# Half groups of down products in other places of a tile of up products

## The chip, the cores and the metric

The kernel runs on one core of one Trainium2 chip. The metric is the device time of one execution in microseconds; the lower the better. A time of the kernel before is the median of several executions, and one more execution was taken with the hardware profiler.

## The reference

The program is a two-layer trunk on 528 tokens (16 meta tokens and 512 real ones) of width 1024: a sparse attention layer, a differential attention layer, and behind each of them the same gated ConvFFN. The change lies in the ConvFFN alone:

```python
def conv_ffn(h, w_up, conv_w, conv_b, w_down):
    Tp = h.shape[1]
    u = h @ w_up
    up = jnp.pad(u, ((0, 0), (CONV_W - 1, 0), (0, 0)))
    c = conv_b + sum(up[:, j:j + Tp] * conv_w[j] for j in range(CONV_W))
    gate, val = jnp.split(c, 2, axis=-1)
    return (jax.nn.silu(gate) * val) @ w_down
```

Here w_up is 1024 x 5632 and w_down 2816 x 1024, all in float32.

## The kernel before

Everything is held with features on the partitions and tokens along the free axis. Every float32 product is made of three matmuls, from an upper and a lower part of each operand: upper times upper, lower times upper, upper times lower. The upper part is a cast by ScalarE (line 168, "hi"), the lower part the remainder, by VectorE (line 176, "lo").

A ConvFFN goes over 22 tiles f of 128 gate and 128 value columns of w_up. Tiles 0 and 1 are computed plainly. Tiles 2 to 21 are computed by up_pair, one after the other, which makes the gate and value columns for both halves of the tokens with seven products instead of eight (a scheme of Strassen's kind, from sums of weights, S12 and S34, and sums of inputs, TT). Each product is twelve matmuls of 264 columns (258 in layer 1), all on line 1240. In the order of the text they are P1 (line 1267, into g0), P5 (1272, into g1), P6 (1278, into v0), P2 (1282, into g0), P3 (1295, into v0), P4 (1299, into g1) and P7 (1307, into v0). g and v are tiles of 1024 columns in PSUM; g0 and v0 lie below column 512, g1 and v1 from it on. g and v take turns in two buffers, so the next tile's g takes the buffer of this tile's.

Between the products, other engines move partial sums: ScalarE copies g0 to v0 behind P1 (line 1270) and g1 to p behind P5 (1274); VectorE writes v0 + p to g1 behind P6 (1279) and to v1 behind P3 (1296). Behind P4 convolve reads g (ScalarE line 1328, then two steps of VectorE, line 1331), and behind P7 it reads v.

The finished tiles of the hidden layer are multiplied by w_down in groups, as soon as four of them are there: a group is one of eight output blocks of 128 rows times four hidden tiles. It comes in two halves. A half group is twelve matmuls of 256 and 272 columns in layer 0 and six of 512 columns in layer 1 (line 1374, into a PSUM tile dn). Behind the second half ScalarE copies dn to y (line 1409), and POOL issues a DMA that adds y to h in memory (line 1410). The function down_slots gives each group a slot: a late one in tiles 4 to 19 (the generator b), or a mid one in tiles 5 to 20 (the generator a). Each next(a) issues one half, and the third next(a) the copy and the DMA.

The order on TensorE, VectorE and ScalarE is the order of the text here, since up_pair is emitted under manual_schedule. Every engine runs its own queue in that order and waits by semaphores where another engine's result is needed, or a buffer that another one still uses.

Weights come through two objects: wt for the up weights and their sums, ws (wsm) for the down weights and the last quarter of the value weight. Each has three buffers for raw, for hi and for lo. early casts a coming unit on ScalarE, late makes its lower part on VectorE, done says that a unit is used up, and each of them may let SP issue the next load (line 115).

Of the kernel before, what the change touches and what calls it, by code (L numbers as in the profile page):

```python
# [229 lines left out]
def mm_cost(n):  # L230
    return n / 2400 + 0.003


class Trunk:
# [929 lines left out]
    def ffn(self, l):  # L1164
# [4 lines left out]
        wt, ws, x = self.wt, self.wsm, self.next_x  # L1169
# [5 lines left out]
        with self.pool("fp") as fp:  # L1175
# [61 lines left out]
            def product(out, w, wk, xs, xk, c0, first=True):  # L1237
                for k in range(4):
                    for p, (wi, xi) in enumerate(((0, 0), (0, 1), (1, 0))):
                        nc.tensor.matmul(out, w[wi][:, wk + k, :], xs[xi][:, xk + k, c0:c0 + N],  # L1240
                                         start=(first and k == 0 and p == 0), stop=(k == 3 and p == 2), skip_group_check=not first)
                    self.pe(3 * mm_cost(N))
                    self.poll()

            def up_pair(f):

                x0, x1 = x[0][2:], x[1][2:]
                off = 512 - mid
                more = f + 1 < NF
                n3, ns = wt.taken, ws.taken
                a, b = ((z.get(f) and down(*z[f])) or iter(()) for z in (at_mid, at_late))
                g = ps.tile([128, 1024], F32, tag="sp", name="g")
                g0, g1 = g[:, off + st0:512], g[:, 512:512 + N]
                for i in range(ns, ns + (f in at_mid) + (f in at_late) + 1):  # L1260
                    ws.early(i)
                before = rest.pop(f - 1, iter(()))
                next(before, None)
                while ws.half:
                    ws.late()
                G, S12 = wt.take(), wt.take()
                product(g0, G, 0, x0, 0, st0)
                v = ps.tile([128, 1024], F32, tag="sp", name="v")
                v0, v1 = v[:, off + st0:512], v[:, 512:512 + N]
                nc.scalar.copy(v0, g0)  # L1270
                next(before, None)
                product(g1, S12, 0, TT[0], 0, 0)
                p5 = fp.tile([128, 264], F32, tag="p", name="p5", bufs=2)[:, :N]
                nc.scalar.copy(p5, g1)
                if more:
                    wt.sum()
                next(a, None)
                product(v0, S12, 4, TT[1], 0, 0, False)
                nc.vector.tensor_tensor(g1, v0, p5, op=OP.add)  # L1279
                if more:  # L1280
                    wt.sum()
                product(g0, G, 4, x0, 4, st0, False)
                wt.done()
                wt.done()
                wt.early(n3 + 3)
                wt.late()
                wt.early(n3 + 4)
                next(a, None)
                next(a, None)
                if f in at_mid:  # L1290
                    ws.done()
                if f + 1 in at_mid:
                    ws.early(ws.taken + (f in at_late) + 1)
                S34 = wt.take()
                product(v0, S34, 0, TT[2], 0, 0, False)
                nc.vector.tensor_tensor(v1, v0, p5, op=OP.add)
                wt.late()
                ws.late()
                product(g1, S34, 4, x1, 4, mid - 264, False)
                wt.done()  # L1300
                convolve(g, f, 0, off)
                wt.early(n3 + 5)
                wt.late()
                next(b, None)
                nc.scalar.activation(conv[0][:, :n], conv[0][:, :n], AF.Silu)
                A22 = ws.take()
                product(v0, A22, 0, TT[3], 0, 0, False)
                convolve(v, f, 1, off)
                next(b, None)
                if f in at_late:  # L1310
                    ws.done()
                ws.done()
                rest[f] = finish_pair(f, conv[0], conv[1], b)
# [3 lines left out]
            def finish_pair(f, c, t, b):  # L1317
                nc.vector.tensor_tensor(c[:, :n], c[:, :n], t[:, :n], op=OP.mult)
                next(b, None)
                yield  # L1320
                split_acts(f, c)
                yield

            def convolve(u, f, e, off=240):
                j = f + NF * e
                w0, w1, w2, b = (par[:, cb + 44 * q + j:cb + 44 * q + j + 1] for q in range(4))
                t = conv[e] = fp.tile([128, T], F32, tag=f"c{e}", name=f"c{e}", bufs=2)
                nc.scalar.activation(t[:, :n], u[:, off + t0:off + T], AF.Identity, bias=b, scale=w2)
                for d, w in ((1, w1), (2, w0)):
                    z = d if l == 0 else 0  # L1330
                    nc.vector.scalar_tensor_tensor(t[:, z:n], u[:, off + t0 + z - d:off + T - d], w, t[:, z:n],  # L1331
                                                   op0=OP.mult, op1=OP.add)
# [66 lines left out]
            def down(p, m):  # L1399
                f0, f1 = self.PARTS[p]  # L1400
                t, w = new(), ws.take()
                for k in range(f1 - f0):
                    if k == (f1 - f0) // 2:
                        yield
                    block(t, w, f0 + k, k, cols, k == 0, k == f1 - f0 - 1)
                yield
                y = fp.tile([128, T], F32, tag="y", name="y", bufs=2)
                for c0, c1, o in cols:
                    nc.scalar.copy(y[:, c0:c1], part(t, c0, c1, o))  # L1409
                nc.gpsimd.dma_start(self.h[m][:, t0:T], y[:, :n], accum_op=OP.add)  # L1410
                yield
# [34 lines left out]
            at_late, at_mid = self.down_slots()  # L1446
# [9 lines left out]
            with self.tc.manual_schedule(engines=ENGINES):  # L1456
                for f in range(self.PLAIN, NF):
                    up_pair(f)
                for _ in rest.pop(NF - 1):
                    pass  # L1460
# [479 lines left out]
```

## Time and profile before

| | |
|---|---|
| runs of the kernel before | 1418.61, 1424.5 and 1425.96 us, median 1424.5 us |
| the profiled execution | 1420.5 us, of which the span of the program is 1418.7 us |
| busy over the span | TensorE 92%, VectorE 73%, ScalarE 51%, POOL 24% |
| granted clock of TensorE, mean over the span | 0.975 of full speed |
| chain that ended last | TensorE 79%, VectorE 12%, ScalarE 5% of the span |
| tiles by up_pair | from about 300 to 640 us (layer 0) and from about 1046 to 1380 us (layer 1) |

Matmuls overlap in the pipeline: a matmul's row lasts about 0.28 us, while the next one starts 0.12 us after it. So a pause of TensorE is read best from start to start; the idle time that the profile gives in brackets is shorter, since it counts from the end of the last row.

### The profile page before, as it was taken

What the parts mean: (1) busy time and instruction counts of PE and PEld (TensorE: products, weight loads), DVE (VectorE), ACT (ScalarE), POOL (GpSimd) and SP (SyncE); (2) the same over time, 40 slices, a digit from 0 to 9 for tenths busy, and PEclk for the clock granted to TensorE, in tenths of its full rate; (3) what the DMA queues carried; (4) which work ended last, traced back from release to release, by engine and by line L of the source; (5) the groups of instructions that cost most, each with busy time, mean ns of one, the idle gap of its engine ahead of it and who ended that gap; (6) DMA issues with size and microseconds to landing.
All of it is one profiled execution on the core that took longest, in us unless ns stands there. A gap on an engine that the chain in (4) does not pass through costs nothing.

```text
span 1418.7 us, 25157 instructions
## 1 busy us (share of the span) xinstructions
PE 1303.5 (92%) x9688; PEld 1239.2 (87%) x9688; DVE 1033.2 (73%) x2030; ACT 723.1 (51%) x1426; POOL 343.4 (24%) x398
## 2 busy tenths in 40 slices
PE   5999899888999999989899999999888999999988
PEld 4999889887999999989799999989887888888886
DVE  6599876788777777766757777775888777777763
ACT  4453555565555555544435655654564555555541
POOL 3404443400000000003454543444500000001100
PEclk9999899999999999999899999989999999999999
DMA  7312221222444444433223222213222444444432
GB/s 229 116 60 84 75 84 58 82 83 59 123 119 120 121 122 122 112 82 101 66 79 93 66 72 76 61 34 89 76 82 75 127 120 119 119 120 127 111 78 93
DMA packets 58519, 136.03 MB, mean 96 GB/s; under 512 B 7216, under 2 KB 16736, under 8 KB 58400
## 3 DMA queue, kind: packets, MB, share of 16 engines
q1 hardware_dynamic: 48432, 114.57, 25.6%
q0 software_dynamic: 9968, 19.87, 8.2%
q8 instruction: 76, 1.25, 0.4%
q14 instruction: 43, 0.35, 0.1%
HBM read 112.46 MB, written 4.91 MB: 83 GB/s over the span
## 4 chain that ended last, share of the span: by engine, by line
PE 79%; DVE 12%; ACT 5%; issue 3%; DMA 1%; POOL 1%; SPq 0%; ACTq 0%; DVEq 0%; POOLq 0%
PE lin L306 21%; PE g L1240 17%; PE dn L1374 17%; PE v L1240 12%; DVE c L1331 2%; PE stq L681 1%; PE pv L1119 1%; PE pv L1745 1%; DVE g L1279 1%; DVE lo L176 1%; ACT v L1270 1%; PE linh L306 1%; PE sa L1024 1%; ACT hi L168 1%; DVE xl L630 1%
## 5 line engine op out<-in xcount | busy, mean ns | idle before, releaser
L306 PE MATMUL lin<-xh,hi 128*128 128x256 f32 (+3 forms) x928 | 273.5, 300 | 13.0 <-DVE ht L547 5.9
L306 PE MATMUL lin<-xl,hi 128*128 128x256 f32 (+3 forms) x928 | 274.0, 296 | 2.3 <-DVE xl L630 2.1
L306 PE MATMUL lin<-xh,lo 128*128 128x256 f32 (+3 forms) x928 | 273.5, 296 | 0.0
L168 ACT CAST hi<-raw 128x1024 fp32r<-128x1024 f32 (+3 forms) x225 | 181.7, 823 | 168.4 <-PE v L1240 81.9
L1410 POOL DMA_DIRECT2D ht<-y x64 | 55.8, 872 | 623.2 <-ACT y L1409 615.9
L306 PEld LDWEIGHTS lin<-xh,hi 128*128 128x128 f32 (+1 forms) x928 | 180.7, 197 | 16.8 <-ACT xh L656 8.4
L176 DVE TENSOR_TENSOR lo<-raw,hi 128x512 fp32r<-128x512 f32 (+3 forms) x196 | 179.0, 928 | 19.8 <-ACT hi L168 16.9
L306 PEld LDWEIGHTS lin<-xl,hi 128*128 128x128 f32 (+1 forms) x928 | 182.6, 197 | 4.0 <-DVE xl L630 3.7
L306 PEld LDWEIGHTS lin<-xh,lo 128*128 128x128 f32 (+1 forms) x928 | 182.5, 197 | 0.0
L1240 PE MATMUL g<-xh,hi 128*128 128x264 f32 (+1 forms) x480 | 140.7, 293 | 30.8 <-DVE g L1279 24.1
L1374 PE MATMUL dn<-al,hi 128*128 128x256 f32 (+2 forms) x528 | 142.6, 320 | 0.0
L1374 PE MATMUL dn<-ah,lo 128*128 128x256 f32 (+2 forms) x528 | 142.3, 321 | 0.0
L1374 PE MATMUL dn<-ah,hi 128*128 128x256 f32 (+2 forms) x528 | 142.2, 321 | 0.0
L1240 PE MATMUL v<-Th,lo 128*128 128x264 f32 (+1 forms) x480 | 136.2, 284 | 0.0
L1240 PE MATMUL v<-Tl,hi 128*128 128x264 f32 (+1 forms) x480 | 136.0, 283 | 0.0
L1240 PE MATMUL v<-Th,hi 128*128 128x264 f32 (+1 forms) x480 | 135.8, 283 | 0.0
L1240 PE MATMUL g<-xh,lo 128*128 128x264 f32 (+1 forms) x480 | 135.8, 283 | 0.0
L1240 PE MATMUL g<-xl,hi 128*128 128x264 f32 (+1 forms) x480 | 135.7, 283 | 0.0
L1240 PEld LDWEIGHTS g<-xh,hi 128*128 128x128 f32 x480 | 90.4, 188 | 40.9 <-DVE g L1279 32.5
L168 ACT CAST hi<-S 128x1024 fp32r<-128x1024 f32 x80 | 83.5, 1043 | 49.5 <-PE g L1240 48.1
L176 DVE TENSOR_TENSOR lo<-S,hi 128x1024 fp32r<-128x1024 f32 x80 | 97.3, 1216 | 0.0
L1374 PEld LDWEIGHTS dn<-ah,lo 128*128 128x128 f32 x528 | 89.1, 188 | 7.5
(301 smaller groups left out, 3304.0 us busy)
## 6 DMA issues: line engine op xcount, KB each, us to landing
raw<-w_up SPq DMA_DIRECT2D x88, 512.0 KB, 3.6
raw<-w_down SPq DMA_DIRECT2D x64, 256.0 KB, 3.2
ht<-y POOLq DMA_DIRECT2D x32, 264.0 KB, 3.6
raw<-w_in SPq DMA_DIRECT2D x16, 512.0 KB, 3.5
raw<-w_kv SPq DMA_DIRECT2D x16, 512.0 KB, 3.6
ht<-y POOLq DMA_DIRECT2D x32, 256.0 KB, 3.6
raw<-w_down SPq DMA_DIRECT2D x16, 384.0 KB, 3.2
nb<-nbias SPq DMA_DIRECT2D x16, 264.0 KB, 2.7
```

The source lines that it names most:

```text
L168: nc.scalar.copy(hi[:, :n, :m], src)
L176: eng.tensor_tensor(lt[:, :n, :m], src, hi[:, :n, :m].bitcast(F32), op=OP.subtract)
L306: i = self.nc.tensor.matmul(o, w[wi][:, kw + k, :m], x[s][xi][:, kx + k, c0:HN[s]], start=(first and p == 0), stop=(last and p == 2))
L630: i = eng.tensor_tensor(xl[:, m, o:o + n], xfs[m][:, :n], xh[:, m, o:o + n].bitcast(F32), op=OP.subtract)
L681: self.nc.tensor.matmul(st[:, c:c + 2], sq[:, c0:c0 + 128], rhs, start=True, stop=True)
L1024: nc.tensor.matmul(s, q[:, c0:c0 + 128], k[:, k0:k1], start=(p == 0), stop=(p == 2))
L1119: nc.tensor.matmul(pv[:, :4 * nq], v[:, c, :], pp[:, :, :nq], start=(ci == 0 and p == 0), stop=(ci == nch - 1 and p == 2))
L1240: nc.tensor.matmul(out, w[wi][:, wk + k, :], xs[xi][:, xk + k, c0:c0 + N], start=(first and k == 0 and p == 0), stop=(k == 3 and p == 2), ...
L1270: nc.scalar.copy(v0, g0)
L1331: nc.vector.scalar_tensor_tensor(t[:, z:n], u[:, off + t0 + z - d:off + T - d], w, t[:, z:n], op0=OP.mult, op1=OP.add)
L1374: nc.tensor.matmul(part(t, c0, c1, o), w[wi][:, k, :], acts[f][ai][:, c0:c1], start=(first and p == 0), stop=(last and p == 2))
L1410: nc.gpsimd.dma_start(self.h[m][:, t0:T], y[:, :n], accum_op=OP.add)
```

## The change

A half group of the mid slot, which was issued between P5 and P6, is now issued between P1 and P5. The other half, which was issued between P2 and P3, is now issued between P6 and P2, and with it goes what followed it: the copies of dn to y, the done of the group's weights, and the cast of the next mid group's weights (ws.early). The lower part of these weights (ws.late) is made there too. Tiles without a mid group (2 to 4 and 21) keep their order on TensorE.

```diff
--- before.py
+++ after.py
@@ -1269,33 +1269,33 @@
                 v0, v1 = v[:, off + st0:512], v[:, 512:512 + N]
                 nc.scalar.copy(v0, g0)
                 next(before, None)
+                next(a, None)
                 product(g1, S12, 0, TT[0], 0, 0)
                 p5 = fp.tile([128, 264], F32, tag="p", name="p5", bufs=2)[:, :N]
                 nc.scalar.copy(p5, g1)
                 if more:
                     wt.sum()
-                next(a, None)
                 product(v0, S12, 4, TT[1], 0, 0, False)
                 nc.vector.tensor_tensor(g1, v0, p5, op=OP.add)
                 if more:
                     wt.sum()
+                next(a, None)
+                next(a, None)
+                if f in at_mid:
+                    ws.done()
+                if f + 1 in at_mid:
+                    ws.early(ws.taken + (f in at_late) + 1)
+                    ws.late()
                 product(g0, G, 4, x0, 4, st0, False)
                 wt.done()
                 wt.done()
                 wt.early(n3 + 3)
                 wt.late()
                 wt.early(n3 + 4)
-                next(a, None)
-                next(a, None)
-                if f in at_mid:
-                    ws.done()
-                if f + 1 in at_mid:
-                    ws.early(ws.taken + (f in at_late) + 1)
                 S34 = wt.take()
                 product(v0, S34, 0, TT[2], 0, 0, False)
                 nc.vector.tensor_tensor(v1, v0, p5, op=OP.add)
                 wt.late()
-                ws.late()
                 product(g1, S34, 4, x1, 4, mid - 264, False)
                 wt.done()
                 convolve(g, f, 0, off)
```

On TensorE, in layer 0, the end of P1 (matmuls into g from xl and xh) and what follows it. Before:

```order
L1240 MATMUL g_4871<-xl0_3497,hi_4763 128x264
L1240 MATMUL g_4871<-xh0_3496,lo_4764 128x264
L1240 MATMUL g_4871<-Th0_3425,hi_4769 128x264
L1240 MATMUL g_4871<-Tl0_3426,hi_4769 128x264
L1240 MATMUL g_4871<-Th0_3425,lo_4770 128x264
```

Now:

```order
L1240 MATMUL g_4871<-xl0_3497,hi_4785 128x264
L1240 MATMUL g_4871<-xh0_3496,lo_4786 128x264
L1374 MATMUL dn_4908<-ah_3707,hi_4767 128x256
L1374 MATMUL dn_4907<-ah_3707,hi_4767 128x272
L1374 MATMUL dn_4908<-al_3708,hi_4767 128x256
```

Behind P1 stood P5 (from Th and Tl); now a half group stands there.

On TensorE, in the same tile, the end of P6 (matmuls into v) and what follows it. Before:

```order
L1240 MATMUL v_4901<-Tl1_3428,hi_4769 128x264
L1240 MATMUL v_4901<-Th1_3427,lo_4770 128x264
L1240 MATMUL g_4871<-xh0_3496,hi_4763 128x264
L1240 MATMUL g_4871<-xl0_3497,hi_4763 128x264
L1240 MATMUL g_4871<-xh0_3496,lo_4764 128x264
```

Now:

```order
L1240 MATMUL v_4901<-Tl1_3428,hi_4791 128x264
L1240 MATMUL v_4901<-Th1_3427,lo_4792 128x264
L1374 MATMUL dn_4908<-ah_3990,hi_4767 128x256
L1374 MATMUL dn_4907<-ah_3990,hi_4767 128x272
L1374 MATMUL dn_4908<-al_3991,hi_4767 128x256
```

Behind P6 stood P2; now the second half group stands there, and P2 behind it.

On ScalarE, from the copy behind P5 to convolve of g (the cast from raw 128x1024 is the next tile's G, the one from S its S12, the one from raw 128x512 the next mid group's down weight). Before:

```order
L1274 COPY p_4513<-g 128x264
L168 CAST hi<-raw 128x1024
L168 CAST hi<-S_4515 128x1024
L1409 COPY y<-dn 128x256
L1409 COPY y<-dn 128x272
L168 CAST hi<-raw 128x512
L1328 ACTIVATE c_4617<-g,par 128x528
```

Now:

```order
L1275 COPY p_4527<-g 128x264
L1409 COPY y<-dn 128x256
L1409 COPY y<-dn 128x272
L168 CAST hi<-raw 128x512
L168 CAST hi<-raw 128x1024
L168 CAST hi<-S_4529 128x1024
L1328 ACTIVATE c_4617<-g,par 128x528
```

The copies to y and the cast of the down weight have moved ahead of the casts of G and S12.

On VectorE, from the sum behind P6 to convolve of g. Before:

```order
L1279 TENSOR_TENSOR g<-v,p_4513 128x264
L141 TENSOR_TENSOR S_4545<-raw,S_4515 128x512
L142 TENSOR_TENSOR S_4545<-raw 128x512
L176 TENSOR_TENSOR lo<-raw,hi 128x1024
L1296 TENSOR_TENSOR v<-v,p_4513 128x264
L176 TENSOR_TENSOR lo<-S_4515,hi 128x1024
L176 TENSOR_TENSOR lo<-raw,hi 128x512
L1331 SCALAR_TENSOR_TENSOR c_4617<-g,par,c_4617 128x527
```

Now:

```order
L1279 TENSOR_TENSOR g<-v,p_4527 128x264
L141 TENSOR_TENSOR S_4545<-raw,S_4529 128x512
L142 TENSOR_TENSOR S_4545<-raw 128x512
L176 TENSOR_TENSOR lo<-raw,hi 128x512
L176 TENSOR_TENSOR lo<-raw,hi 128x1024
L1297 TENSOR_TENSOR v<-v,p_4527 128x264
L176 TENSOR_TENSOR lo<-S_4529,hi 128x1024
L1331 SCALAR_TENSOR_TENSOR c_4617<-g,par,c_4617 128x527
```

The lower part of the down weight has moved from the place ahead of convolve to the place ahead of G's lower part; line 1296 is line 1297 in the changed file. On SP the same loads stand in another order: two of w_up and two of w_down in turn were issued in pairs, and are now issued one of a kind after one of the other. POOL's order is the same.

## Rows read from the trace of the kernel before

**Rows 1.** Busy time in two stretches; columns: stretch, length, PE, PEld, DVE, ACT, POOL, clock, DMA.
```profile
450.00:500.00 50.00, 46.69 (x373) 45.42 (x372) 37.61 (x53) 25.75 (x45) 5.18 (x6) 1.00 0.47 126
1200.00:1250.00 50.00, 47.22 (x317) 43.10 (x317) 36.81 (x53) 26.20 (x40) 4.35 (x5) 1.00 0.48 127
```

**Rows 2.** Who waited for whom on PE, whole span: us in total, times, longest.
```profile
PE g L1240 <- ACT v L1270: 27.5, 40, 1.7
PE g L1240 <- DVE g L1279: 24.1, 40, 0.8
```

**Rows 3.** Timeline of PE, layer 0, P1 to P5: start, length, instruction, idle before.
```profile
422.12 0.28 PE L1240 MATMUL g<-xh,lo 128*128 128x264 f32 x1
422.90 0.39 PE L1240 MATMUL g<-Th,hi 128*128 128x264 f32 x1 [0.50 <-ACT v L1270]
423.12 0.29 PE L1240 MATMUL g<-Tl,hi 128*128 128x264 f32 x1
```

**Rows 4.** Timeline of PE, layer 0, P6 to P2.
```profile
427.30 0.28 PE L1240 MATMUL v<-Th,lo 128*128 128x264 f32 x1
428.18 0.39 PE L1240 MATMUL g<-xh,hi 128*128 128x264 f32 x1 [0.60 <-DVE g L1279]
428.41 0.28 PE L1240 MATMUL g<-xl,hi 128*128 128x264 f32 x1
```

**Rows 5.** Timeline of PE, layer 1: a half group, P6 to P2, P1 to P5.
```profile
1200.56 0.39 PE L1374 MATMUL dn<-ah,hi 128*128 128x512 f32 x1
...
1201.95 0.28 PE L1240 MATMUL v<-Th,hi 128*128 128x258 f32 x1
...
1203.28 0.28 PE L1240 MATMUL v<-Th,lo 128*128 128x258 f32 x1
1204.15 0.39 PE L1240 MATMUL g<-xh,hi 128*128 128x258 f32 x1 [0.60 <-DVE g L1279]
...
1215.49 0.28 PE L1240 MATMUL g<-xh,lo 128*128 128x258 f32 x1
1216.26 0.39 PE L1240 MATMUL g<-Th,hi 128*128 128x258 f32 x1 [0.49 <-ACT v L1270]
```

**Rows 6.** Timeline of PE, layer 0, tile 3: P2 to P3, P5 to P6.
```profile
328.07 0.28 PE L1240 MATMUL g<-xh,lo 128*128 128x264 f32 x1
328.19 0.28 PE L1240 MATMUL v<-Th,hi 128*128 128x264 f32 x1
...
338.68 0.29 PE L1240 MATMUL g<-Th,lo 128*128 128x264 f32 x1
338.81 0.28 PE L1240 MATMUL v<-Th,hi 128*128 128x264 f32 x1
```

**Rows 7.** Timeline of ACT, layer 0, the tile of rows 4, behind P6.
```profile
427.49 1.05 ACT L168 CAST hi<-raw 128x1024 fp32r<-128x1024 f32 x1 [2.45 <-PE v L1240]
...
431.29 0.66 ACT L1409 COPY y<-dn 128x256 f32<-128x256 f32 x2 [0.41 <-PE dn L1374]
431.83 0.63 ACT L168 CAST hi<-raw 128x512 fp32r<-128x512 f32 x1
434.34 0.79 ACT L1328 ACTIVATE c<-g,par 128x528 f32<-128x528 f32 x1 [1.88 <-PE g L1240]
```

**Rows 8.** Timeline of DVE, layer 0, the same tile and the next one's L1279.
```profile
427.69 0.44 DVE L1279 TENSOR_TENSOR g<-v,p 128x264 f32<-128x264 f32 x1 [1.76 <-PE v L1240]
...
429.24 1.22 DVE L176 TENSOR_TENSOR lo<-raw,hi 128x1024 fp32r<-128x1024 f32 x1
432.88 0.44 DVE L1296 TENSOR_TENSOR v<-v,p 128x264 f32<-128x264 f32 x1 [2.42 <-PE v L1240]
...
434.36 0.69 DVE L176 TENSOR_TENSOR lo<-raw,hi 128x512 fp32r<-128x512 f32 x1
435.17 1.57 DVE L1331 SCALAR_TENSOR_TENSOR c<-g,par,c 128x527 f32<-128x527 f32 x2
...
445.39 0.44 DVE L1279 TENSOR_TENSOR g<-v,p 128x264 f32<-128x264 f32 x1 [1.74 <-PE v L1240]
```

## The prediction

> **What bounds the kernel now.** I began with the busy time by stretch, because the change touches only the two runs of up_pair tiles. In a stretch in the middle of each, TensorE is busy 46.69 and 47.22 of 50 us at a granted clock of 1.00 (2.4 GHz), while VectorE is busy 37.61 and 36.81, ScalarE 25.75 and 26.20, and the DMA engines under half [rows 1]. PE is the engine that sets the pace, and its clock is already at the upper level. What is left to gain there is idle time of PE, so the second view is who waited for whom. Two waits stand out, both once in each of the 40 up_pair tiles: PE waits for ScalarE's copy of g0 into v0 (line 1270), 27.5 us, and for VectorE's sum into g1 (line 1279), 24.1 us [rows 2].
>
> The third view, the timeline of PE, tells where these two stand and what they really cost. The first is between P1 and P5: the last matmul of P1 starts at 422.12, the first of P5 at 422.90 [rows 3]. The second is between P6 and P2: 427.30 and 428.18 [rows 4]. Undisturbed, the next matmul of this width starts 0.12 us after the one before [rows 6]. The half groups of down products wait for neither, but the queue of PE is in program order, and they stand behind P5 and behind P2. The pauses look like dependences of the tile g as a whole: P5 writes g1 while ScalarE reads g0, and P2 writes g0 while VectorE writes g1. The reader should see that work which could run stands right behind each pause.
>
> **What one tile loses.** Layer 0, first pause: 0.78 us instead of 0.12, so 0.66; and the second matmul of P5 follows after 0.22 (422.90 to 423.12) instead of 0.12, another 0.10. Together 0.76 us [rows 3]. Second pause: 0.88 less 0.12 is 0.76, and 0.23 less 0.12 is 0.11 behind it, together 0.87 us [rows 4]. Layer 1: 0.77 (1215.49 to 1216.26) and 0.87 (1203.28 to 1204.15) instead of 0.12, with the same 0.10 and 0.11 behind them: 0.75 and 0.86 us [rows 5]. That is 1.63 us in a tile of layer 0 and 1.61 in one of layer 1. A cross-check from the whole tile: VectorE's sum recurs after 17.70 us (427.69 to 445.39) [rows 8]; the tile issues seven products and four half groups, 132 matmuls, which at 0.1215 us (0.12 to 0.13 in [rows 6]) need 16.04. The difference is 1.66, so these two pauses are all that PE loses in such a tile.
>
> **Half groups moved, PE.** A half group with its twelve matmuls of 264 columns on average takes 12 x 0.12 = 1.46 us in layer 0, and 1.39 (1200.56 to 1201.95) in layer 1 [rows 5]. Put behind P1, it fills the first pause: P5 could start 0.78 after P1's last matmul began, and now comes 0.12 + 1.46 = 1.58 after it, with 0.80 to spare (layer 1: 1.51 against 0.77). Put behind P6, it fills the second: P2 could start after 0.88 and comes after 1.58, 0.70 to spare. Both pauses go in full, in the tiles that have a mid group: tiles 5 to 20, sixteen in each layer. Tiles 2 to 4 and 21 keep theirs.
>
> **What loses its cover.** P6 now follows P5 directly, and P3 follows P2. The kernel before has both neighbours already, in tiles without a mid group, and there they cost nothing: P3 starts 0.12 behind P2's last matmul and P6 0.13 behind P5's [rows 6]. P6 needs only the copy of g0 that P5 had to wait for, and P3 needs VectorE's sum, which ends a half group and a product earlier. I cost both at zero.
>
> **ScalarE and VectorE, in program order.** On ScalarE the copies of y and the cast of the 512-wide down weights now stand ahead of the casts of the next G and S12, and on VectorE that low half (512 wide) ahead of the low half of G and of L1297. Counted from the start of P6's last matmul: the moved half group's last matmul starts at 1.46 and y follows 0.2 later; y takes 0.66, the 512-wide cast 0.63, the cast of G 1.05 [rows 7], which ends at 4.0. The low half of G, 1.22, ends at 5.2 and L1297, 0.44, at 5.7 [rows 8] (P3 has ended by 4.8). P7, the first to need L1297, starts after five groups, 5 x 1.46 + 0.12 = 7.4: 1.7 us to spare. The low half of S12, 1.22, ends at 6.9. ScalarE's first step of convolve for g needs P4, whose last matmul starts at 4 x 1.46 = 5.8, so with 0.3 of signalling and its 0.79 [rows 7] it ends at 6.9 also; VectorE's two steps, 1.57 [rows 8], end at 8.5. The next P1, which takes g's buffer, starts at 7 x 1.46 + 0.12 = 10.3: 1.8 to spare. In the kernel before the same sum stood equally far from its P1, because VectorE then did the 512-wide low half right ahead of it (434.36, and convolve at 435.17) [rows 8]. In tile 20, which has no late group, P7 comes 1.46 earlier, at 5.9; but there is no 512-wide cast or low half either, so L1297 only waits for P3 and ends at 4.8 + 0.4 = 5.2. I cost ScalarE and VectorE at zero too.
>
> **The queues of DMAs.** SP now issues its four loads of a tile in alternation, up, down, up, down, because ws.done comes earlier. No load changes size or buffer, and each of their waits is for a VectorE step whose order on VectorE is the same as SP's. The second up weight is issued behind the low half of G, which moves back by about two us in the tile; the sums that use it come in the next tile, behind P5. DMA engines run at 0.47 to 0.48 of their time [rows 1] and would go to 0.52 in the shorter tile. I cost this at zero. POOL's accumulating DMA follows y in both versions, and y moves with the group.
>
> **The sum.** 16 x 1.63 + 16 x 1.61 = 51.8 us. Against the profiled execution, 1420.5 us: 1368.7. The median of the three runs is 4.0 us above that execution; with part of this I predict **1370 us**. Bounds: nothing excludes that some tenth of a microsecond a tile comes back (0.2 x 32 = 6 us), and what phase the later stages' clock falls into may add or take some 5 us; I allow 1361 to 1382 for this case alone.
>
> **The rule that speaks against it.** The rows show PE idle with ScalarE's copy and VectorE's sum named as what ended it, 40 times each [rows 2]. The Trainium skill (PSUM — Partial Sum Buffer, section "PSUM bank collisions raise a hardware error") asks that two engines be kept apart by bank and quadrant, not more. The halves g0 and g1 lie on either side of column 512 of g, one 2 KiB bank each, so by that rule neither pause has to exist, moving other work into it would bring nothing, and the time would stay at 1420.5. The trace decides against that here: the waits are in the program as built, whatever the chip would need.
>
> **The rivals.**
> 1. *Only one pause goes.* If the copy of g0 comes late, because VectorE's convolve of the last tile ends later in the shorter tile and holds v's buffer, or P2 still waits, one of the two stays. It would leave 32 x 0.87 = 27.8 or 32 x 0.76 = 24.3 us: 1393 or 1396. For it speaks that VectorE goes from 37 in 50 us to some 41; against it the spare of 0.7 to 0.8 us at both places. Chance 0.07.
> 2. *No change.* The pause is not in g's tile but in something that comes with any start of P5 or P2 (for this the rule above would speak), or moves whole to P3 and P6. Against it: these neighbours ran without a pause [rows 6]. 1417 to 1424. Chance 0.04.
> 3. *Slower.* ScalarE's queue is in order, and the y copies and the 512-wide cast now hold up the casts of G and S12, and through VectorE L1297 and convolve. If that chain is later than I laid it out by more than the 1.8 us that P1 has to spare, PE waits there; from 1.8 + 1.6 = 3.4 us on the change costs more than it gives. At 4 us it would be 32 x 0.6 = 19 us slower, 1440. It would take a down weight that lands late in SP's new order, for instance. Chance 0.04.
>
> My forecast keeps 0.85. The range for 8 in 10 takes in its bounds and reaches towards rival 1: **1360 to 1392**. About 0.5% (7 us) is what a measurement of this kernel can tell from no change; faster by more than that: 0.92, within it 0.04, slower 0.04.
>
> **What would show it.** In the profile after, the wait of PE for line 1270 should be left with 8 times of 40 (tiles 2 to 4 and 21), and the same for line 1279; L1279 should recur after some 16.1 us in layer 0 and 1.6 us sooner than before in layer 1; the stretch of rows 1 should show PE busy above 49 of 50 us. PE's wait for convolve (line 1331) should not grow. I am wrong if a new wait of PE for line 1296's successor 1297, for a cast, or for line 1331 appears in tiles 5 to 20, or if P5 still starts behind a pause.

## The result, and the profile after

The changed kernel takes **1370.5 us** (median of four runs, 1369.62 to 1372.38); the kernel before, run beside it, 1423.8 us (1418.61 to 1425.96). The ratio is 0.9633, with a 95% interval of 0.9604 to 0.9661. The profiled execution has a span of 1367.8 us where the one before had 1418.7.

In the rows PE is TensorE, ACT ScalarE and DVE VectorE. The waits of PE come first, as in [rows 2]. Here are the three costliest ones of g, over the whole span: us in total, times, longest.

```profile
PE g L1240 <- ACT v L1270: 11.3, 8, 1.7
...
PE g L1240 <- DVE c L1331: 6.6, 6, 1.1
...
PE g L1240 <- DVE g L1279: 4.7, 8, 0.6
```

Both waits of [rows 2] fell from 40 times to 8, which is tiles 2 to 4 and 21 of both layers. The wait for convolve (line 1331) is what it was; the kernel before had:

```profile
PE g L1240 <- DVE c L1331: 6.6, 6, 1.1
```

No new wait on g or v took the place of the two.

Busy time in two stretches in the middle of the two runs of up_pair tiles, which answer to [rows 1] (columns: stretch, length, PE, PEld, DVE, ACT, POOL, clock, DMA share, GB/s):

```profile
450.00:500.00 50.00, 50.00 (x413) 50.00 (x412) 40.91 (x58) 27.50 (x49) 5.22 (x6) 1.00 0.53 134
1150.00:1200.00 50.00, 50.00 (x349) 46.73 (x348) 41.01 (x59) 26.91 (x43) 5.22 (x6) 1.00 0.56 145
```

PE is busy in all of the 50 us. What is left in these tiles is matmuls at the upper clock level (1.00, 2.4 GHz), 132 of them in 16.06 us or 0.122 us each: nothing is left there for the order of the work to win. VectorE is at 41 of 50, as rival 1 had it, and still it holds up nothing.

The timeline of PE in one tile of layer 0 (start, length, instruction; an idle time would stand in brackets), from the end of P1 to the next tile's P1:

```profile
416.05 0.29 PE L1240 MATMUL g<-xh,lo 128*128 128x264 f32 x1
416.18 0.40 PE L1374 MATMUL dn<-ah,hi 128*128 128x256 f32 x2
...
417.40 0.41 PE L1374 MATMUL dn<-ah,lo 128*128 128x256 f32 x2
417.64 0.29 PE L1240 MATMUL g<-Th,hi 128*128 128x264 f32 x1
417.77 0.29 PE L1240 MATMUL g<-Tl,hi 128*128 128x264 f32 x1
...
419.00 0.29 PE L1240 MATMUL g<-Th,lo 128*128 128x264 f32 x1
419.12 0.28 PE L1240 MATMUL v<-Th,hi 128*128 128x264 f32 x1
...
420.47 0.29 PE L1240 MATMUL v<-Th,lo 128*128 128x264 f32 x1
420.59 0.40 PE L1374 MATMUL dn<-ah,hi 128*128 128x256 f32 x2
...
421.82 0.40 PE L1374 MATMUL dn<-ah,lo 128*128 128x256 f32 x2
422.05 0.28 PE L1240 MATMUL g<-xh,hi 128*128 128x264 f32 x1
...
423.38 0.29 PE L1240 MATMUL g<-xh,lo 128*128 128x264 f32 x1
423.50 0.29 PE L1240 MATMUL v<-Th,hi 128*128 128x264 f32 x1
...
427.89 0.28 PE L1240 MATMUL v<-Th,hi 128*128 128x264 f32 x1
...
430.81 0.28 PE L1240 MATMUL g<-xh,hi 128*128 128x264 f32 x1
```

Read it against [rows 3] and [rows 4]. P5 starts 1.59 us after P1's last matmul (416.05 to 417.64), with twelve matmuls in between, and its second matmul follows after 0.13 us, not 0.22: it waits for nothing. P2 starts 1.58 us after P6's last (420.47 to 422.05), also at once. The new neighbours P5 and P6 (419.00, 419.12) and P2 and P3 (423.38, 423.50) are 0.12 us apart, like those of [rows 6].

ScalarE and VectorE in the same tile, behind P6 (their timelines; here the bracket is the idle time before and what ended it):

```profile
422.13 0.66 ACT L1409 COPY y<-dn 128x256 f32<-128x256 f32 x2 [2.42 <-PE dn L1374]
422.67 1.58 ACT L168 CAST hi<-raw 128x512 fp32r<-128x512 f32 x2
...
426.64 0.79 ACT L1328 ACTIVATE c<-g,par 128x528 f32<-128x528 f32 x1 [1.44 <-PE g L1240]
```

```profile
420.86 0.44 DVE L1279 TENSOR_TENSOR g<-v,p 128x264 f32<-128x264 f32 x1 [1.00 <-PE v L1240]
...
425.43 0.43 DVE L1297 TENSOR_TENSOR v<-v,p 128x264 f32<-128x264 f32 x1
...
427.47 1.57 DVE L1331 SCALAR_TENSOR_TENSOR c<-g,par,c 128x527 f32<-128x527 f32 x2 [0.48 <-ACT c L1328]
...
436.94 0.44 DVE L1279 TENSOR_TENSOR g<-v,p 128x264 f32<-128x264 f32 x1 [0.99 <-PE v L1240]
```

The row of the casts (422.67, x2) is two casts in a row, the down weight's and G's. L1279 recurs after 16.08 us (420.86 to 436.94), where it was 17.70 [rows 8].

One number serves all the comparisons below: the time from one tile's L1279 to the next one's, as a mean of the 15 tiles in the middle of each run (from tile 5's to tile 20's). And one sum: the time from tile 2's L1279 to tile 21's, of both layers together.

| kernel | period, layer 0 | period, layer 1 | both runs of tiles | median of all |
|---|---|---|---|---|
| before | 17.71 | 17.25 | 644.9 | 1424 |
| after | 16.06 | 15.63 | 592.8 | 1370.5 |
| first half group moved alone | 16.92 | 16.51 | 620.5 | 1391.2 |
| second half group moved alone | 16.83 | 16.39 | 617.1 | 1390.0 |
| TensorE's order alone | 16.06 | 15.63 | 592.7 | 1370.6 |
| before, P5 in its own bank | 16.95 | 16.50 | 616.2 | 1389.8 |
| change, P5 in its own bank | 16.06 | 15.63 | 588.2 | 1364.8, again 1360.1 |
| the same, VectorE's sum first | 16.06 | 15.63 | 584.1 | 1356.4 |
| change, copy of g0 three times | 16.13 | 15.78 | 608.2 | 1384.1 |
| before, copy of g0 three times | 18.48 | 18.04 | 680.6 | 1456.8 |

Within a run the 15 single periods of a layer lie within 0.1 us of each other (one of 17.95 us in the kernel before excepted), and kernels with the same order on TensorE have the same mean to 0.01 us, so differences of a tenth of a microsecond a tile can be read from the means. The medians can't be read so finely, for a reason that comes out below.

### The profile page after: what moved, and what is told of

Same layout as the page of the kernel before. It is cut to its first block, busy times and chain, and to the rows that moved or that the text cites. A ratio compares the mean times of both kernels' runs of the same rounds, so it can differ in the third digit from the quotient of the medians.

```text
span 1367.8 us, 25126 instructions
## 1 busy us (share of the span) xinstructions
PE 1284.9 (94%) x9688; PEld 1233.5 (90%) x9688; DVE 1032.4 (75%) x2030; ACT 716.7 (52%) x1426; POOL 343.3 (25%) x398
## 4 chain that ended last, share of the span: by engine, by line
PE 80%; DVE 11%; ACT 4%; issue 2%; POOL 1%; DMA 1%; SPq 0%; ACTq 0%; DVEq 0%; POOLq 0%
PE lin L306 22%; PE dn L1374 18%; PE g L1240 17%; PE v L1240 12%; DVE c L1331 2%; PE pv L1745 1%; PE stq L681 1%; PE pv L1119 1%; PE linh L306 1%; DVE lo L176 1%; DVE xl L630 1%; ACT hi L168 1%; PE sa L1024 1%; PE stk L671 1%; PE sb L1671 1%
## 5 line engine op out<-in xcount | busy, mean ns | idle before, releaser
L168 ACT CAST hi<-raw 128x512 fp32r<-128x512 f32 (+3 forms) x225 | 178.8, 824 | 90.9 <-PE lin L306 47.6
L176 DVE TENSOR_TENSOR lo<-raw,hi 128x1024 fp32r<-128x1024 f32 (+3 forms) x196 | 179.1, 929 | 55.1 <-ACT hi L168 52.1
L1240 PE MATMUL g<-xh,hi 128*128 128x264 f32 (+1 forms) x480 | 137.3, 286 | 11.3 <-DVE c L1331 6.6
L1374 PEld LDWEIGHTS dn<-ah,hi 128*128 128x128 f32 x528 | 88.8, 188 | 5.7 <-ACT hi L168 1.1
```

Of the source, the lines that this page charges most:

```text
L168: nc.scalar.copy(hi[:, :n, :m], src)
L176: eng.tensor_tensor(lt[:, :n, :m], src, hi[:, :n, :m].bitcast(F32), op=OP.subtract)
L1374: nc.tensor.matmul(part(t, c0, c1, o), w[wi][:, k, :], acts[f][ai][:, c0:c1], start=(first and p == 0), stop=(last and p == 2))
```

## The experiments

**The two halves apart.** The theory is two pauses that are filled independently; the rival is that the gain hangs on one of them, or on both together. In the first kernel only the half group between P1 and P5 is moved, and what follows P2 stays as it was (against the kernel before):

```diff
                 next(before, None)
+                next(a, None)
                 product(g1, S12, 0, TT[0], 0, 0)
...
-                next(a, None)
                 product(v0, S12, 4, TT[1], 0, 0, False)
```

> Only the first half group moves (P1, half, P5, P6, P2, half, P3). Theory (each pause is covered by the work put into it, and the two gains add up): the 32 first pauses of 0.76 us go, 24.3 us, so 1423.8 - 24 = about 1399.5 us; PE's wait for line 1270 falls to 8 times, that for 1279 stays at 40. Rival (PE only trades one pause for another, or both must go before anything is won): 1415 to 1424 us, with a longer pause ahead of P2 or a new one ahead of P6.

In the second only the other half group goes, from behind P2 to behind P6, with the copies of y and the cast and the lower part of the down weight (against the kernel before):

```diff
                 if more:
                     wt.sum()
+                next(a, None)
+                next(a, None)
+                if f in at_mid:
+                    ws.done()
...
                 product(g0, G, 4, x0, 4, st0, False)
...
                 wt.early(n3 + 4)
-                next(a, None)
-                next(a, None)
...
```

> Only the second half group moves (P1, P5, half, P6, half, P2, P3), with the y copies and the down weight's cast and lower part as in the change. Theory: the 32 second pauses of 0.87 us go, 27.8 us, so about 1396 us; PE's wait for line 1279 falls to 8 times, that for 1270 stays at 40. Rival: 1415 to 1424 us, the pause having moved to P3.

Measured: 1391.2 us, ratio 0.9783 (0.9761 to 0.9805), and 1390.0 us, ratio 0.9772 (0.9751 to 0.9794). The waits of PE, of the first and of the second kernel:

```profile
PE g L1240 <- DVE g L1279: 23.9, 40, 0.6
...
PE g L1240 <- ACT v L1270: 11.1, 8, 1.7
```

```profile
PE g L1240 <- ACT v L1270: 27.0, 40, 1.7
...
PE g L1240 <- DVE g L1279: 4.7, 8, 0.6
```

Each half takes away its own pause, 40 to 8, and leaves the other as it was. In the table the first is worth 0.79 and 0.74 us a tile (expected 0.76 and 0.75), the second 0.88 and 0.86 (expected 0.87 and 0.86). Together that is 1.66 and 1.60, and the whole change gave 1.64 and 1.62: the two add up. The medians are some 8 and 6 us below what I expected, though the runs of tiles gave 24.4 and 27.8 us, as expected (644.9 less 620.5 and less 617.1). In the profiled executions another 6.3 and 3.2 us were gained in stages that neither edit touches; they are taken up below.

**The order of the other engines.** Only the half groups stand as in the changed kernel, against which the edit is shown. The copies of y, the done, and the cast and lower part of the down weight stay behind P2 and P3, so that ScalarE, VectorE, POOL and SP keep the order of before:

```diff
                 next(a, None)
-                next(a, None)
-                if f in at_mid:
-                    ws.done()
-                if f + 1 in at_mid:
-                    ws.early(ws.taken + (f in at_late) + 1)
-                    ws.late()
                 product(g0, G, 4, x0, 4, st0, False)
...
                 wt.early(n3 + 4)
+                next(a, None)
+                if f in at_mid:
+                    ws.done()
...
```

> TensorE's order is that of the change, ScalarE's, VectorE's and SP's stay as in the kernel before: the y copies, the done of the group's weights, and the next mid group's cast and lower part are issued where they were. Theory (their move costs and brings nothing): as the change, 1370.5 us within 3. Rival (part of the gain, or a hidden cost, lies in the order of the other engines): more than 4 us away from 1370.5, below it if the y copies ahead of G's cast cost something, above it if they help.

Measured: 1370.6 us, ratio 0.9635 (0.9613 to 0.9657), the same periods to 0.01 us. What moved on the other engines and in the loads costs nothing and brings nothing. All of the gain is TensorE's order.

**Is it g's tile, or the chip?** P5 is written to a PSUM tile of its own in the kernel before, with the half groups in their old places. The product is the same and has the same operands; only its output lies elsewhere, and the copy to p reads it there:

```diff
-                product(g1, S12, 0, TT[0], 0, 0)
+                q1 = g1 if f == self.PLAIN else ps.tile([128, 512], F32, tag="one", name="q")[:, :N]
+                product(q1, S12, 0, TT[0], 0, 0)
...
-                nc.scalar.copy(p5, g1)
+                nc.scalar.copy(p5, q1)
```

> The order of the kernel before; but P5 writes a 512-column PSUM tile of its own and p is copied from there (tile 2 excepted). No half group moves. Theory (P5 waits for line 1270 only since g0 and g1 are one tile of the program): P5 follows P1 without a pause, 32 x 0.76 = 24 us; in tiles 3, 4 and 21 of each layer the pause of about 2.0 us moves to P6 and shrinks by one product, 1.46 us, 6 x 1.46 = 9 us. Together 33 us: 1391 us. Rival (the pause comes with any start of P5, whatever it writes): 1424 us.

Measured: 1389.8 us, ratio 0.9774 (0.9751 to 0.9796). The timeline of PE, P1 to P5 (now into q) in a middle tile:

```profile
418.08 0.29 PE L1240 MATMUL g<-xh,lo 128*128 128x264 f32 x1
418.20 0.29 PE L1240 MATMUL q<-Th,hi 128*128 128x264 f32 x1
```

The copy of g0 in the same tile, on ScalarE:

```profile
418.45 0.36 ACT L1270 COPY v<-g 128x264 f32<-128x264 f32 x1 [0.46 <-PE g L1240]
```

P6 to P2 in tile 3:

```profile
324.32 0.28 PE L1240 MATMUL v<-Th,lo 128*128 128x264 f32 x1
326.22 0.39 PE L1240 MATMUL g<-xh,hi 128*128 128x264 f32 x1 [1.61 <-DVE g L1280]
```

With nothing put into it, the first pause is gone: P5 starts 0.12 us behind P1. A middle tile gains 0.76 and 0.75 us, what the moved half group gained there. P5 is under way while ScalarE copies g0. So the pause was no need of P5 or of its operands; it came with the place that P5 writes. That the program guards g as a whole is the likely reading, since g0 and g1 lie in two banks already; the edit changes tile and bank at once, and does not part the two. Tiles 3 and 4 are another matter. Their first pause is the longest (1.7 us of idle time), and yet they gained just 0.4 us each (14.41 and 14.39 to 14.00 in layer 0): their second pause grew from 0.88 to 1.90 us, and P6 now starts 0.5 us behind P5's last matmul, waiting for the same copy. The median is close to the 1391 us that I expected by luck: the tiles gave 28.7 us (644.9 to 616.2) of the 33. The timeline of VectorE in tile 3 shows the sum that it waits for (line 1280 here):

```profile
325.13 0.69 DVE L138 TENSOR_TENSOR S<-S,raw 128x512 f32<-128x512 f32 x1
325.74 0.43 DVE L1280 TENSOR_TENSOR g<-v,p 128x264 f32<-128x264 f32 x1
```

P6 finishes early now, and VectorE, which has the same work as ever ahead of the sum, is not there yet: a weight sum (lines 137 and 138, 0.69 us each) stands before it, and the sum starts 1.42 us after P6's last matmul does (324.32 to 325.74). In the middle tile shown above, that weight sum was over at 421.89, and P6's last matmul started at 422.50.

**The change and the bank together, and VectorE's order beside it.** The same edit was made in the changed kernel, where it should only help tiles 3, 4 and 21:

> The change, and P5 in a PSUM tile of its own as well. Theory: in tiles 5 to 20 nothing is left to win; in tiles 3, 4 and 21 of each layer the pause ahead of P5 (about 2.0 us) moves to P6 and shrinks by one product, 6 x 1.46 = 9 us: 1370.5 - 9 = about 1361.5 us. Rival (the pauses of tiles without a mid group are set by the chain of ScalarE and VectorE behind them, so that a shorter pause at P5 comes back at P1 of the next tile): 1366 to 1371 us.

Measured: 1364.8 us, ratio 0.9586 (0.9558 to 0.9614). The runs of tiles shrink by 4.6 us: tiles 3 and 4 gain 0.4 us each, as above, and tile 21, where no weight sum is made, 1.44. So I had counted 4.4 us too much for the tiles, and the median is 3.3 us above what I expected. Then, besides, VectorE makes the sum of line 1280 first in tiles without a mid group (the edit against the kernel just measured):

```diff
-                if more:
+                if more and f in at_mid:
                     wt.sum()
...
                 nc.vector.tensor_tensor(g1, v0, p5, op=OP.add)
                 if more:
                     wt.sum()
+                    if f not in at_mid:
+                        wt.sum()
```

> The changed kernel with P5 in a bank of its own, and besides in tiles without a mid group (2 to 4 and 21) VectorE makes the sum behind P6 (line 1280) ahead of both halves of the weight sums, not between them. In tiles 3 and 4 of the kernel with P5's own bank the pause P6 to P2 had grown from 0.88 to 1.90 us, with the two steps of a weight sum (0.69 us each) ahead of line 1280 on VectorE. Theory: those two steps are what the pause waits for; it falls back to some 0.9 us in tiles 2 to 4 of both layers, 6 x 1.0 us, and the stretch from tile 2's sum to tile 21's shrinks by 4 us or more per two layers (tile 2's own pause lies ahead of it): 1359 to 1361 us beside 1364.8. Rival: the pause is set by the chain through convolve of the tile before and the copy of g0 to v0 (lines 1332 and 1270), which ends late whatever VectorE does in between: unchanged, 1364 to 1366.

> The changed kernel with P5 in a bank of its own once more, unchanged, beside the kernel with VectorE's sum first, so that the two are timed on the same chip: 1364.8 us again, within 3 us.

Measured on one chip: 1356.4 us, ratio 0.9524 (0.9495 to 0.9552), and without the edit 1360.1 us, ratio 0.9551 (0.9524 to 0.9579). The first matmul of P2 in tile 3, without the edit and with it:

```profile
328.16 0.39 PE L1240 MATMUL g<-xh,hi 128*128 128x264 f32 x1 [1.65 <-DVE g L1280]
```

```profile
323.19 0.39 PE L1240 MATMUL g<-xh,hi 128*128 128x264 f32 x1 [0.60 <-DVE g L1280]
```

The pause is back to 0.60 us of idle time, as in [rows 4], in tiles 3 and 4 of both layers: four times 1.0 us, and the runs of tiles are 4.1 us shorter. Tile 2's pause had never grown, so two of the six that I counted were not there. The kernel that was run again came out 4.7 us below its first median, more than the 3 us that I allowed. The intervals of the two ratios overlap, and the tiles settle it. The median lies 14 us below the changed kernel's, of which the tiles explain 8.7 (592.8 to 584.1).

**How much room is left.** ScalarE copies g0 to v0 three times in place of once, in the changed kernel and in the kernel before. If the copy is on the path, that costs what two more copies take; if a half group covers it, the cost is what goes beyond the room that I worked out (0.80 and 0.74 us):

```diff
-                nc.scalar.copy(v0, g0)
+                for _ in range(3):
+                    nc.scalar.copy(v0, g0)
```

> The change, with ScalarE's copy of g0 into v0 (line 1270) issued three times instead of once: 0.6 to 0.7 us more ahead of P5. Theory (the half group covers it, 0.80 us to spare in layer 0 and 0.74 in layer 1): tiles 5 to 20 stay as they are, the 8 other tiles pay 0.6 to 0.7 us each, about 5 us: 1375.5 us. Rival (the cover is not there, the gain has another source): 40 x 0.65 = 26 us, 1396 us.

> The kernel before, with the copy of g0 into v0 three times. Theory (P5 waits for this copy in every tile): 40 x 0.65 = 26 us more, 1450 us. Rival (the copy is not what P5 waits for): 1424 us.

Measured: 1384.1 us, ratio 0.9723 (0.9697 to 0.9748), and 1456.8 us, ratio 1.0241 (1.0206 to 1.0275). In the kernel before, each middle tile is longer by 0.77 and 0.79 us; in the changed one by 0.06 and 0.14. So the half group covers 0.71 us of the two copies in layer 0 and 0.65 in layer 1; the room that I gave was right but for some 0.1 us. That 0.1 is mostly P5's second matmul: in a middle tile of layer 0 the first one is on time (425.78, 0.12 us behind the half group's last), and the second follows after 0.21 us (425.99). Both medians are 7 to 9 us above my expectation, and this time it is the tiles. In the kernel before two copies cost 0.78 us where I had counted 0.65, some 4 us over 32 tiles. And in both kernels tiles 3, 4 and 21, where nothing covers the copy, grew by up to 2.35 us where two copies explain 0.8. The timeline of PE in tile 3 of the changed kernel with three copies, and the busy time of two stretches behind such a pause (columns as above):

```profile
327.45 0.39 PE L1240 MATMUL g<-Th,hi 128*128 128x264 f32 x1 [2.50 <-ACT v L1271]
...
328.05 0.38 PE L1240 MATMUL g<-Tl,hi 128*128 128x264 f32 x1
328.22 0.42 PE L1240 MATMUL g<-Th,lo 128*128 128x264 f32 x1
...
331.30 0.38 PE L1240 MATMUL v<-Tl,hi 128*128 128x264 f32 x1
331.52 0.28 PE L1240 MATMUL v<-Th,lo 128*128 128x264 f32 x1
```

```profile
328.00:331.40 3.40, 3.40 (x18) 3.40 (x17) 1.98 (x3) 0.38 (x1) 0.00 (x0) 0.51 0.00 0
...
619.40:622.80 3.40, 2.80 (x24) 2.59 (x22) 1.15 (x2) 1.19 (x3) 0.00 (x0) 1.00 0.41 116
```

Behind an idle time of 2.50 us the matmuls restarted at the usual pace, but from 328.05 on the clock was at the lower level (0.51, where 0.50 is 1.2 GHz) and they started 0.22 us apart, where 0.12 is usual. Between 328.05 and 331.52 there are 16 starts in 3.47 us; at 0.12 us each they would have taken 1.9. So the clock cost some 1.5 us, which is what was missing in tile 3's period (2.35 less 0.8). The second stretch lies behind the pause of tile 21 in layer 0, 2.49 us of idle time before 618.95, and there the clock stayed at 1.00.

**The stages that nothing touches.** The medians strayed from the tiles by up to 8 us. Up to tile 2's sum in layer 0 all these kernels issue the same 2080 matmuls. That stage in the kernel with the second half group alone, and in the changed one with P5's own bank:

```profile
0.00:308.70 308.70, 278.01 (x2080) 263.97 (x2080) 239.26 (x598) 159.79 (x353) 109.25 (x129) 0.98 0.31 96
```

```profile
0.00:317.00 317.00, 284.84 (x2080) 270.35 (x2080) 239.24 (x597) 159.90 (x353) 109.36 (x129) 0.95 0.31 94
```

VectorE and ScalarE have the same busy time; TensorE's clock was granted at 0.98 in one and at 0.95 in the other, and the stage took 8.3 us longer. These two are the ends of eleven profiled executions (before 311.7, after 312.4). The changed kernel with P5's own bank had 317.0 and, run again, 313.6. The stretch from tile 21's sum in layer 0 to tile 2's in layer 1 goes from 412.6 us (clock 0.95) to 419.8 us (0.93). That the clock comes out differently is shown; what sets it in these stages was not tried.

## Why the prediction was right

**The two pauses.** The sum was 51.8 us; the runs of tiles shrank by 52.1 (644.9 to 592.8). Per tile it was 1.63 and 1.61 forecast, 1.64 and 1.62 measured, and the two terms hold apart as well (0.76 and 0.87). Measuring from start to start mattered: the bracketed idle time of [rows 3] and [rows 4], 0.50 and 0.60 us, gives 1.10 a tile and would have missed a third. The slower second matmul behind a wait (0.22 and 0.23) belongs to the price too, and it is gone. That the median came within 1 us of the forecast is luck, though: the other stages alone move a run by several microseconds. The sum over the tiles is what bears the mechanism out.

**Lost cover and new neighbours at zero.** P6 behind P5 and P3 behind P2 start after 0.12 us, and PE has no idle time in the middle stretches. (Of [rows 6], the second pair is from tile 4, not tile 3; the reading is the same.)

**ScalarE, VectorE and the loads at zero.** Counted from the start of P6's last matmul (420.47), the chain came as laid out: y at 1.66 (forecast 1.46 + 0.2), convolve's first step ends at 6.96 (6.9), VectorE's part of it at 8.57 (8.5), the next P1 starts at 10.34 (10.3), and L1297 ends at 5.39 (5.7), 2.0 us ahead of P7 at 7.42 (7.4). TensorE's order alone gave the same time, so the zero is measured, not only argued.

**The room at P5** was 0.80 and 0.74 us by the sum, and by the experiment some 0.1 less. Nothing decided on that. The room at P2, 0.70 us by the sum, was not tried, but the rows bear it out: VectorE's sum ends 0.75 us ahead of P2 (421.30, 422.05), where it ended 0.05 us ahead before (428.13 in [rows 8], 428.18 in [rows 4]).

**The rule against it.** With P5 in a tile of its own the pause went away, which is what the bank rule of the Trainium skill (PSUM — Partial Sum Buffer, section "PSUM bank collisions raise a hardware error") says of the chip: ScalarE may read one bank while TensorE writes another. The trace agrees: P5 started 0.12 us behind P1 (418.08, 418.20), and the copy of g0 ran from 418.45 to 418.81, with P5's matmuls going on. It did not follow that the time stays: the kernel before does wait, whatever the chip would need, and as long as it does, filling the pause and removing its cause are worth the same (0.76 a tile). For P2 and VectorE's sum the cause was not tried.

**The rivals.** Rival 1 needed one wait left at 40 times; both stand at 8, and the kernels with one half only show what it would have looked like, 1390 to 1391 us. Rival 2 is out by the ratio and by P5's start. Rival 3 needed P1 late by more than its room; the wait for line 1331 is unchanged. The allowance for the clock of other stages was needed in kind: outside the tiles the profiled execution lost 1.2 us (52.1 gained there, 50.9 in the span), and other kernels moved by up to 8.

## What to carry to other kernels

When an in-order engine stands still at the same place in each repetition, look for work that stands behind the place and does not depend on it, and measure the pause from start to start, with the slower restart. If the wait is on a tile of which each side uses one half, try two tiles: for P5 that removed the wait with nothing put in. Then see what the other engine still has ahead of the next step that is waited for. Compare variants by the period of the repetition itself when stages elsewhere vary by more than the difference.

## What was not expected of the hardware

A pause can cost more than its length. Of the six places in the changed kernel with three copies where TensorE stood idle for 2.4 to 2.5 us at P5, the clock fell to the lower level behind five, and stayed at 1.00 behind one; in the kernel before with three copies it fell behind four of the six. With one copy the same places have an idle time of 1.6 to 1.7 us, and the clock stayed at 1.00 behind all six, before and after the change. Two copies of some 0.4 us each thus cost up to 2.35 us in a tile.

And the same instructions of the first stage took 308.7 to 317.0 us, with a clock of 0.98 to 0.95, while middle tiles at full clock repeat within some 0.1 us. A gain of under half a per cent can't be told by the median of so few runs here, though the trace shows it plainly.
